# The mixing layer of a decoder block: products with tokens on partitions instead of features

## The chip, the cores and the metric

The kernel runs on one core of a Trainium2 chip. The metric is the device time of one execution in microseconds. TensorE is called PE, VectorE DVE, ScalarE ACT, GpSimdE POOL, and SyncE, which issues most transfers, SP. Each engine works through its own instructions in order.

## The reference

One decoder layer for 256 tokens of 1024 channels in float32: a feed-forward, a mixing layer, a second feed-forward, a last norm. What concerns us is the mixing layer:

```python
n = rmsnorm(h, mix_norm[l])
z = n @ w_in[l]                      # q, k, v, u, gv: 512 columns each
attn = moba_attention(q, k, v)       # one block of 256 keys: plain causal attention, 8 heads of 64
zg = gelu(z[..., 3 * A_WIDTH:])
gm = chunked_spatial_gating(u, gv, gmlp_ln_g[l], gmlp_ln_b[l], gmlp_w_s[l], gmlp_b_s[l])
                                     # u * (w_s @ layernorm(gv) + b_s) in chunks of 128 tokens, 8 groups
gates = sigmoid(n @ w_gate[l] + b_gate[l])                       # 2048 columns
merged = gates[..., :D] * (attn @ w_branch_attn[l]) + gates[..., D:] * (gm @ w_branch_gmlp[l])
h = h + merged @ w_out[l]
```

## The kernel before

Every large product is taken as three: each float32 operand is split into a rounded high part (a cast on ACT) and a remainder (a subtraction on DVE), and high x high, high x low and low x high are summed in PSUM. The weights come from DRAM in units of 1 MB, each in two halves (`raw`, seven buffers), and are split into `w` (four buffers), so a unit can be split up to three units ahead of PE. A half costs ACT one cast and DVE one subtraction of 1024 columns.

Two forms of product occur.

- Tokens stationary (`chunk`, `value`): a block of 128 features x 128 tokens is loaded, and 512 columns of weights move past it. The result has tokens on partitions. Each k-block gives three products of 512 columns for each of the two token halves. The feed-forwards, v and gv are made so.
- Weights stationary (`by_weights`, `by_passes`): a block of 128 x 128 weights is loaded and the tokens move: their high and low part together as 512 columns (`mm_high`, L165), then the high part alone, 256 columns, past the low weights (`mm_low`, L170). The result has features on partitions, in two halves of a bank; `collect` copies one on ACT and adds the other on DVE. Queries, keys, u (12 blocks of 128 features) and the gates (16 blocks) are made so, since what follows wants features on partitions.

`down_features` is the weights-stationary product that ends the first feed-forward and the mixing layer (`acc`): the last two units are taken feature block by feature block, so that DVE can add each to the residual `h`, ACT and DVE can split the next layer's input, and PE can go on with the next layer.

The factor 1/rms of each token is found late, in `token_factors`, so it is applied to the results. With features on partitions this needs a row of factors (`rows_of`, two transposes on PE) and a multiplication on DVE for each block.

PE and SP run in the order in which the program is written. ACT and DVE follow the written order inside `with in_order()` blocks (the ends of `down_features` and the start of the second feed-forward); between them a scheduler orders them. The mixing layer stands so: v, token factors, gv, queries and keys, u, scores (`sc`, L622), spatial product (`mix`, L607), 13 gate blocks, attention product (`po`), 3 gate blocks, branches (`pb`, L723 to L737), output product. The softmax's probabilities go through DRAM (`on_way`) to get keys onto partitions: `to_keys` writes them after gate block 1 and `by_keys` loads them after gate block 4.

Of the kernel before, what the change touches and what calls it, by code (L numbers as in the profile page):

```python
# [18 lines left out]
P = 128  # L19
# [26 lines left out]
def block_kernel(ctx, tc, t, out):  # L46
# [148 lines left out]
    def collect(to, ps, n=1):  # L195

        lo = tmp.tile([P, S], F32, tag="lo", name="lo")
        nc.scalar.copy(lo, ps[:, S:])
        high = ps[:, :S]
        if n > 1:  # L200
            high, lo = (x.rearrange("p (n c) -> p n c", n=n) for x in (high, lo))
        nc.vector.tensor_add(to, high, lo)

# [58 lines left out]
    def rows_of(rs, name):  # L262

        ps = bank(f"rows{name}")
        for j in range(NT):
            nc.tensor.transpose(ps[:, j * P:(j + 1) * P], rs[j].to_broadcast([P, P]), ident)
        r = small.tile([P, S], F32, tag="rows", name=f"rowsb{name}", bufs=1)
        nc.scalar.copy(r, ps[:, :S])
        return r

    def weights_of(w, nT, blk):
        c = slice(blk * P, (blk + 1) * P)
        return lambda k: ((w[:, k, 0, c], w[:, k, 1, c]), both_of(nT, k))

    def by_weights(name, i, nT, blk):

        ps, w = bank(name), unit(i, ALONE)
        by_passes([(ps, weights_of(w, nT, blk))])
        return ps

    HALVES = ((0, 512), (512, 512))

    def down_features(i0, n_units, both_of_k, scale, gain, nT, name, free, behind=()):
# [15 lines left out]
        for i in range(n_units - 2):  # L299
            unit(i0 + i, ALONE if i == n_units - 3 else PAIRED)  # L300
# [14 lines left out]
        for c in range(KB):  # L315
            blocks([c], range(K - 4, K))
# [70 lines left out]

    class Hidden:
# [22 lines left out]
        def leave(self, c):  # L411
            p, e = divmod(c, 2)
            n = 32 * self.blocks(p)
            if e == 0:
                self.way[p] = dram.tile([S, 4, n], F32, name=f"{self.name}way{p}")
            a = CH // n
            nc.sync.dma_start(self.way[p].rearrange("(j p) a n -> p j a n", p=P)[:, :, a * e:a * (e + 1), :],
                              self.turned.pop(c).rearrange("p j (a n) -> p j a n", a=a))

        def arrive(self, p):  # L420
            n = 32 * self.blocks(p)
            self.back[p] = tmp.tile([P, S // 32, n], F32, tag="back", name=f"{self.name}back{p}", bufs=1)
            way = self.way.pop(p).rearrange("(q r) a n -> r q a n", r=32)
            for a in range(4):
                nc.sync.dma_start(self.back[p][32 * a:32 * a + 32], way[:, :, a, :])

        def settle(self, p):
            n = self.blocks(p)
            to = self.aT[:, 4 * p:4 * p + n].rearrange("p k two (q c) -> p two q k c", c=32)
            split(to[:, 0], to[:, 1], self.back.pop(p).rearrange("p q (k c) -> p q k c", c=32))  # L430
# [88 lines left out]
    cols = consts.tile([P, 4 * KB], F32, name="cols")  # L519
    nc.sync.dma_start(cols, t["cols"])  # L520
    bgate, gain2, gain3 = cols[:, :2 * KB], cols[:, 2 * KB:3 * KB], cols[:, 3 * KB:]
    bs = consts.tile([P, GG // 2, P], F32, name="bs")
    for two in range(2):
        nc.sync.dma_start(bs[two * HD:(two + 1) * HD],
                            t["b_s"][two:two + 1].to_broadcast([HD, GG // 2, P]))
# [11 lines left out]
    pv, pgv = {}, {}  # L537

    def value(ps, i0, j, u):
        if u == 0:  # L540
            ps[j] = bank(f"p{units[i0][0]}{j}")
        w = unit(i0 + u)
        tk = slice(j * P, (j + 1) * P)
        for k in range(KB // 2):
            st = tuple(p[:, tk] for p in block_of(nT2, KB // 2 * u + k))
            mm3(ps[j], st, (w[:, k, 0, :], w[:, k, 1, :]), u + k == 0, u == 1 and k == KB // 2 - 1)


    with in_order():
        down_features(f1d, FB // 2, lambda k: hidden.aT[:, k], 0.5, gain2, nT2, "2", "nD", hidden.rest())  # L550
        for u in range(2):
            for j in range(NT):
                value(pv, mv, j, u)
# [3 lines left out]
        gates = mix_a[:, :2 * KB, :]  # L557
        gv = mix_a[:, 2 * KB:2 * KB + 4, :].rearrange("p (j a) t -> p j (a t)", j=NT)
        va = mix_b[:, 0:4, :].rearrange("p (j a) t -> p j (a t)", j=NT)
        uT = mix_b[:, 4:8, :]  # L560
        lng = mix_a[:, 20:22, :].rearrange("p a t -> p (a t)")
        lnb = mix_b[:, 20:22, :].rearrange("p a t -> p (a t)")
        nc.sync.dma_start(lng, t["ln_g"].to_broadcast([P, GW]))
        nc.sync.dma_start(lnb, t["ln_b"].to_broadcast([P, GW]))
        prob = [mix_b[:, 8:12, :].rearrange("p a (b n) -> p (a b) n", b=2), mix_b[:, 12:20, :]]
        for j in range(NT):
            nc.vector.tensor_scalar(va[:, j, :], pv[j], rs2[j], None, op0=ALU.mult)
    for u in range(2):
        for j in range(NT):
            value(pgv, mgv, j, u)  # L570
    rows2 = rows_of(rs2, "2")
    for j in range(NT):
        nc.scalar.activation(gv[:, j, :], pgv[j], AF.Gelu_apprx_tanh, scale=rs2[j])

    def layer_norm(j):
        st = small.tile([P, 6], F32, tag="st", name=f"st{j}")
        nc.vector.bn_stats(st, gv[:, j, :])
        mvr = small.tile([P, 2], F32, tag="mvr", name=f"mvr{j}")
        nc.vector.bn_aggr(mvr, st)
        ve = small.tile([P, 1], F32, tag="ve", name=f"ve{j}")  # L580
        nc.vector.tensor_scalar(ve, mvr[:, 1:2], EPS, None, op0=ALU.add)
        r = small.tile([P, 1], F32, tag="lnr", name=f"lnr{j}")
        nc.gpsimd.tensor_tensor(r, ve, nhalf, op=ALU.pow)
        nc.vector.tensor_scalar(gv[:, j, :], gv[:, j, :], mvr[:, 0:1], r, op0=ALU.subtract, op1=ALU.mult)
        nc.vector.tensor_mul(gv[:, j, :], gv[:, j, :], lng)
        nc.vector.tensor_add(gv[:, j, :], gv[:, j, :], lnb)

    qk = act.tile([P, 2 * (HEADS // 2), S], F32, tag="nC", name="qk")
    qT, kT = qk[:, :4], qk[:, 4:]
    for f in range(8):  # L590
        collect(qk[:, f, :], by_weights(f"pq{f}", mq + f // 2, nT2, f % 2))
        nc.vector.tensor_mul(qk[:, f, :], qk[:, f, :], rows2)
    for j in range(NT):
        layer_norm(j)

    for f in range(4):
        us = tmp.tile([P, S], F32, tag="us", name=f"uz{f}")
        collect(us, by_weights(f"pu{f}", mu + f // 2, nT2, f % 2))
        nc.vector.tensor_mul(us, us, rows2)
# [284 lines left out]
```

## Time and profile before

| | before |
|---|---|
| runs, us | 528.55, 528.67, 528.75 (median 528.67) |
| the profiled execution, us | 528.46 |
| its span in the trace, us | 526.8 |
| up to the mixing layer (0 to 186.87): PE, DVE, ACT busy, us | 185.69, 119.64, 95.55 |
| second feed-forward and end (340.68 to 526.80): PE, DVE, ACT busy, us | 179.93, 115.39, 83.20 |
| DMA in these two stages, GB/s | 258, 212 |

The span is what the trace holds from the first to the last instruction; the execution's own time lies 1.7 us above it. A row of the timeline begins with start and duration in us. A row of groups ends with count, busy us and mean ns of one, then idle time of the engine before it. A row of windows has, after the stretch and its length, the busy us of PE, weight loads, DVE, ACT and POOL, the clock granted to PE, and the DMA's share and GB/s. Rows on transfers end with their size and the us from issue to landing.

### The profile page before, as it was taken

What the parts mean: (1) busy time and instruction counts of PE and PEld (TensorE: products, weight loads), DVE (VectorE), ACT (ScalarE), POOL (GpSimd) and SP (SyncE); (2) the same over time, 40 slices, a digit from 0 to 9 for tenths busy, and PEclk for the clock granted to TensorE, in tenths of its full rate; (3) what the DMA queues carried; (4) which work ended last, traced back from release to release, by engine and by line L of the source; (5) the groups of instructions that cost most, each with busy time, mean ns of one, the idle gap of its engine ahead of it and who ended that gap; (6) DMA issues with size and microseconds to landing.
All of it is one profiled execution on the core that took longest, in us unless ns stands there. A gap on an engine that the chain in (4) does not pass through costs nothing.

```text
span 526.8 us, 7279 instructions
## 1 busy us (share of the span) xinstructions
PE 519.4 (99%) x2668; PEld 441.6 (84%) x2668; DVE 367.0 (70%) x568; ACT 273.0 (52%) x401; POOL 11.5 (2%) x20
## 2 busy tenths in 40 slices
PE   9999999999999999999999999999999999999995
PEld 6888888888888888888888998888888888888884
DVE  6886666675453689978998887799665755575424
ACT  7755354554343367547967545565444453463402
POOL 0010000000000001000000000001000000000002
PEclk9999999999999999999999999999999999999998
DMA  8999597979668229764299645259797879677302
GB/s 318 369 342 318 138 361 257 255 230 277 201 191 298 102 84 338 255 204 160 86 282 347 200 143 181 83 176 340 239 263 259 283 249 329 178 238 233 127 1 80
DMA packets 52419, 118.72 MB, mean 225 GB/s; under 512 B 6816, under 2 KB 26784, under 8 KB 52384
## 3 DMA queue, kind: packets, MB, share of 16 engines
q1 hardware_dynamic: 52096, 117.94, 68.4%
q8 instruction: 21, 0.34, 0.2%
q10 hardware_dynamic: 288, 0.33, 0.2%
q14 instruction: 14, 0.11, 0.1%
HBM read 108.81 MB, written 9.44 MB: 224 GB/s over the span
## 4 chain that ended last, share of the span: by engine, by line
PE 98%; DVE 0%; issue 0%; POOLq 0%; ACT 0%; DVEq 0%; POOL 0%; ACTq 0%
PE f L192 14%; PE f L193 14%; PE f L191 14%; PE acc L165 10%; PE pgate L165 6%; PE acc L170 5%; PE acch L193 4%; PE acch L192 4%; PE acch L191 4%; PE pgate L170 3%; PE pq L165 3%; PE pb L193 1%; PE pb L191 1%; PE pb L192 1%; PE pq L170 1%; PE pu L165 1%
## 5 line engine op out<-in xcount | busy, mean ns | idle before, releaser
L207 DVE TENSOR_TENSOR w<-raw,w 128x1024 fp32r<-128x1024 f32 x180 | 212.8, 1217 | 67.0 <-ACT w L205 66.6
L205 ACT CAST w<-raw 128x1024 fp32r<-128x1024 f32 x180 | 180.3, 1049 | 88.8 <-PE f L193 49.8
L193 PE MATMUL f<-w,n 128*128 128x512 f32 x336 | 130.7, 389 | 0.0
L192 PE MATMUL f<-w,n 128*128 128x512 f32 x336 | 130.7, 389 | 0.0
L191 PE MATMUL f<-w,n 128*128 128x512 f32 x336 | 130.7, 389 | 0.0
L191 PEld LDWEIGHTS f<-w,n 128*128 128x128 f32 x336 | 63.1, 188 | 13.2
L192 PEld LDWEIGHTS f<-w,n 128*128 128x128 f32 x336 | 63.1, 188 | 13.1
L193 PEld LDWEIGHTS f<-w,n 128*128 128x128 f32 x336 | 63.1, 188 | 13.0
L165 PE MATMUL acc<-f1h,w 128*128 128x512 f32 x176 | 43.4, 391 | 0.0
L165 PEld LDWEIGHTS acc<-f1h,w 128*128 128x128 f32 x176 | 31.9, 188 | 5.8
L191 PE MATMUL acch<-w,f2h 128*128 128x512 f32 x84 | 32.7, 389 | 0.0
L192 PE MATMUL acch<-w,f2h 128*128 128x512 f32 x84 | 32.7, 389 | 0.0
L193 PE MATMUL acch<-w,f2h 128*128 128x512 f32 x84 | 32.7, 389 | 0.0
L165 PE MATMUL pgate<-n,w 128*128 128x512 f32 x128 | 32.6, 394 | 0.0
L165 PEld LDWEIGHTS pgate<-n,w 128*128 128x128 f32 x128 | 23.0, 189 | 4.4 <-DVE mixed L629 0.2
L403 ACT ACTIVATE f2s<-f,rstd 128x256 f32<-128x256 f32 x22 | 10.3, 474 | 29.6 <-PE f L193 29.6
L405 DVE SCALAR_TENSOR_TENSOR f2a<-f,rstd,f2s 128x256 f32<-128x256 f32 x22 | 10.5, 476 | 20.9 <-ACT f2s L403 20.9
L170 PEld LDWEIGHTS acc<-f1h,w 128*128 128x128 f32 x176 | 23.5, 190 | 1.5
L170 PE MATMUL acc<-f1h,w 128*128 128x256 f32 x176 | 23.9, 282 | 0.0
L403 ACT ACTIVATE f1s<-f,rstd 128x256 f32<-128x256 f32 x22 | 10.3, 473 | 24.3 <-PE f L193 22.8
L318 DVE SCALAR_TENSOR_TENSOR h<-acc,h 128x256 f32<-128x256 f32 x32 | 13.6, 425 | 10.1 <-PE acc L165 8.1
L192 PEld LDWEIGHTS acch<-w,f2h 128*128 128x128 f32 x84 | 15.8, 188 | 3.3
(166 smaller groups left out, 634.1 us busy)
## 6 DMA issues: line engine op xcount, KB each, us to landing
raw<-in_f SPq DMA_DIRECT2D x84, 512.0 KB, 6.4
raw<-in_f1d SPq DMA_DIRECT2D x22, 512.0 KB, 6.1
raw<-in_f2d SPq DMA_DIRECT2D x22, 512.0 KB, 6.8
raw<-in_gate SPq DMA_DIRECT2D x16, 512.0 KB, 4.6
raw<-in_qk SPq DMA_DIRECT2D x8, 512.0 KB, 6.0
raw<-in_out SPq DMA_DIRECT2D x8, 512.0 KB, 4.7
f1way<-f1t SPq DMA_DIRECT2D x11, 256.0 KB, 6.7
f2way<-f2t SPq DMA_DIRECT2D x11, 256.0 KB, 6.3
```

The lines of the kernel that those rows point to most:

```text
L165: nc.tensor.matmul(ps, st, both.rearrange("p two n -> p (two n)"), start=first, stop=last)
L170: nc.tensor.matmul(ps[:, n:], st, both[:, 0, :], start=False, stop=False)
L191: nc.tensor.matmul(ps, sh, mh, start=first, stop=False)
L192: nc.tensor.matmul(ps, sh, ml, start=False, stop=False)
L193: nc.tensor.matmul(ps, sl, mh, start=False, stop=last)
L205: nc.scalar.copy(hi, src)
L207: nc.vector.tensor_sub(lo, src, hi.bitcast(F32))
L318: nc.vector.scalar_tensor_tensor(h[:, c, :], acc[c][:, q * S:(q + 1) * S], scale, h[:, c, :], op0=ALU.mult, op1=ALU.add)
L403: nc.scalar.activation(sg, ps[j][:, :CH], AF.Silu, scale=rs[j])
L405: nc.vector.scalar_tensor_tensor(a, ps[j][:, CH:], rs[j], sg, op0=ALU.mult, op1=ALU.mult)
```

## The change

All of the mixing layer's input products, and the branches, take the tokens-stationary form with 512 columns of weights moving: seven groups of 512 columns instead of 28 blocks of 128. `collect`, `rows_of`, `by_weights` and `value` go, and the token factor becomes the scale of the instruction that empties PSUM. What is needed with features on partitions is turned: DVE transposes squares of 32 x 32, the result is written to a DRAM tile, and `from_way` reads it back in four transfers, each with another order of blocks; the weights' rows and columns are permuted on the host to match. The first feed-forward's hidden values are turned in this way already (`Hidden`).

- Queries and keys: scaled on ACT, transposed, written (`qk_way`) and read back before the scores. Keys are used as they land, queries after a copy on ACT.
- Gated features: bias, multiplication with u and transpose with tokens on partitions, then `gm_way` and a split into `gmT`. The spatial product has the triangular `w_s` stationary (8 products instead of 16, each 128 columns).
- Gates: one operation on DVE (scale and bias) and a sigmoid on ACT for each 512 columns and token half.
- Merged branches: three pieces of 512, 256 and 256 columns, each multiplied with its gates, added, transposed, turned through `m_way` and split into `mT`. The first is written and read on SP, the others on ACT's queue.
- The probabilities are scaled and transposed by one instruction each for a token half instead of eight or four.
- Order: q, token factors, k, gv, u, scores, spatial, v, gate groups 0, 1, 2, attention, branch piece 0 (gated first), gate group 3, branch pieces 1 and 2, output product. The whole layer stands in `in_order()`, so ACT and DVE keep the written order too.
- `down_features` gets a count `near`: the output product takes only its last unit block by block, and the pieces' last steps run after its first and second unit. The token sums for the second feed-forward come half a chunk later.

```diff
-    mv = add_units("v", 2)
-    mgv = add_units("gv", 2)
-    mq = add_units("qk", 4)
-    mu = add_units("u", 2)
-    mg = add_units("gate", 8)
+    mq, mk, mgv, mu, mv = (add_units(name, 2) for name in ("q", "k", "gv", "u", "v"))
+    mg = add_units("gate", 6)
     mb = len(units)
-    for i in range(2):
-        units.extend([("ba", i), ("bg", i)])
+    units.extend([("bg", 0), ("ba", 0), ("gate", 6), ("gate", 7), ("ba", 1), ("bg", 1)])
...
-        for i in range(n_units - 2):
+        far = n_units - near
+        for i in range(far):
...
+    def from_way(to, way, queue=nc.sync):
+        squares32 = way.rearrange("(q r) a n -> r q a n", r=32)
+        for a in range(4):
+            queue.dma_start(to[32 * a:32 * a + 32], squares32[:, :, a, :])
...
+        def gate(g, ps):
+            c = slice(g * 512, (g + 1) * 512)
+            for j in reversed(range(NT)):
+                nc.vector.scalar_tensor_tensor(gates[:, j, c], ps[j], rs2[j], gates[:, 0, c],
+                                               op0=ALU.mult, op1=ALU.add)
+                nc.scalar.activation(gates[:, j, c], gates[:, j, c], AF.Sigmoid)
...
+        psg = chunk(mg, nT2, "g", 1, [0])
+        by_keys()
+        gm_back = tmp.tile([P, S // 32, P], F32, tag="back", name="gmback", bufs=1)
+        from_way(gm_back, gm_way)
+        chunk(mg, nT2, "g", 1, [1], psg)
+        gate(2, psg)
+        gate(1, chunk(mg, nT2, "g", 2))
...
+        settle_in(gmT, gm_back)
+        aoT, = alloc_T("ao", ("nC",))
+        for hp in range(4):
+            attend(hp)
+        for i, bT in enumerate((gmT, aoT)):
+            for j in range(NT):
+                ps = bank(f"pb{i}{j}")
+                branch(ps, ((i, ALONE), bT), j, *pieces[0])
+                m = gates[:, j, (1 - i) * D:(1 - i) * D + 512]
+                nc.vector.tensor_mul(m, ps, m)
+                if i:
+                    merged(0, j)
...
+            if p == 1:
+                settle(0)
+                leave(1)
+        from_way(m_back[1], m_way[1], nc.scalar)
+        leave(2)
+
+        def second():
+            from_way(m_back[2], m_way[2], nc.scalar)
+            settle(1)
+
+        def third():
+            settle(2)
...
-        down_features(mo, 4, lambda k: both_of(mT, k), 1.0, gain3, nT3, "3", "aT")
+        down_features(mo, 4, lambda k: both_of(mT, k), 1.0, gain3, nT3, "3", "aT", 1, [second, third])
```

ACT before, around the third gate block: a conversion of the gated features (`gm`) stands between the blocks' copies (`lo`), sigmoids (L669) and weight casts (`w`).

```order
L669 ACTIVATE mixed<-gz_2303,cols 128x256
L205 CAST gm_2300<-gm_2337 128x256
L205 CAST w_2505<-raw_0_2145 128x4x256
L198 COPY lo<-pgate_2417 128x256
L205 CAST w_2505<-raw_1_2308 128x4x256
L669 ACTIVATE mixed<-gz_2341,cols 128x256
L205 CAST gm_2300<-gm_2366 128x256
```

ACT in the changed kernel, at the end of gate group 1 (the L619 row is its two sigmoids; `gmback` is what the gated features' reads filled, `po` the attention product):

```order
L193 CAST w_2393<-raw_0_2248 128x2x512
L193 CAST w_2393<-raw_1_2283 128x2x512
L619 ACTIVATE mixed<-mixed 128x512 x2
L193 CAST gm_1771<-gmback 128x8x4x32
L193 CAST ao_2437<-po_2438 128x256
L193 CAST ao_2437<-po_2445 128x256
L193 CAST ao_2437<-po_2452 128x256
```

The four conversions of the gated features are now one, behind the sigmoids of a group that PE ends right before the attention product, whose results are converted next.

SP in the changed kernel, around the loads of the probabilities by key (`on_way`): the weight loads before them wait for buffers that DVE frees.

```order
L137 DMA raw_0_2209<-in_ba 128x1024
L587 DMA on_way_1774<-turned_2186 32x8x256 x4
L690 DMA gmway<-mixed 128x512 x2
L137 DMA raw_1_2244<-in_ba 128x1024
L137 DMA raw_0_2248<-in_gate 128x1024
L137 DMA raw_1_2283<-in_gate 128x1024
L137 DMA raw_0_2287<-in_gate 128x1024
L594 DMA mixed<-on_way_1773 128x1024
L594 DMA mixed<-on_way_1774 128x1024 x2
L362 DMA gmback<-gmway 32x8x128 x4
```

The probabilities' writes and loads keep four weight loads between them as before; the gated features' writes and reads now stand behind each.

ACT in the changed kernel, from the last branch piece into the output product (`mway` are the DRAM tiles of pieces 1 and 2, `mg` the split merged branches, the `w` casts weights of the output product):

```order
L193 CAST mg_2621<-mixed 128x8x4x32
L723 DMA mway_2431<-mt_2433 128x2x256
L362 DMA mixed<-mway_2431 32x8x64 x4
L723 DMA mway_2432<-mt_2434 128x2x256
L193 CAST w_2762<-raw_0_2511 128x1024
L193 CAST w_2762<-raw_1_2549 128x1024
L362 DMA mixed<-mway_2432 32x8x64 x4
L193 CAST mg_2622<-mixed 128x8x2x32
L193 CAST w_2809<-raw_0_2553 128x1024
L193 CAST w_2809<-raw_1_2583 128x1024
L193 CAST mg_2622<-mixed 128x8x2x32
```

Before, ACT issued no transfer here; now ten of them stand in its queue among the casts.

More of the change, by code (lines that the diff above doesn't have):

```diff
@@ L260, in token_factors, with down_features @@
         return [r[:, j:j + 1] for j in range(NT)]
[L262 to L279, printed above, removed]
     HALVES = ((0, 512), (512, 512))
-    def down_features(i0, n_units, both_of_k, scale, gain, nT, name, free, behind=()):
+    def down_features(i0, n_units, both_of_k, scale, gain, nT, name, free, near, behind):
         acc = [bank(f"acc{name}{c}") for c in range(KB)]
@@ L315, in down_features @@
         for c in range(KB):
-            blocks([c], range(K - 4, K))
+            blocks([c], range(2 * far, K))
             for q in range(2):
@@ L535, in block_kernel @@
     nT2 = alloc_T("n2", ("nA", "nB"))
[L537 to L546, printed above, removed]
     with in_order():
[L550 to L553, printed above, removed]
+        down_features(f1d, FB // 2, lambda k: hidden.aT[:, k], 0.5, gain2, nT2, "2", "nD", 2, hidden.rest())
+        psq = chunk(mq, nT2, "q", 0)
         rs2 = token_factors("2")
@@ L556, in block_kernel, with tokens @@
         mix_a, mix_b = mixed[:, :FB], mixed[:, FB:]
[L557 to L562, printed above, removed]
+        def tokens(blocks):
+            return blocks.rearrange("p (j a) t -> p j (a t)", j=NT)
@@ new lines, in block_kernel @@
+        gates = tokens(mix_a[:, :2 * KB])
+        gv, va, ut = tokens(mix_a[:, 16:20]), tokens(mix_b[:, 0:4]), tokens(mix_b[:, 4:8])
+        lng, lnb = (mix[:, 20:22].rearrange("p a t -> p (a t)") for mix in (mix_a, mix_b))
+        prob = [mix_b[:, 8:12, :].rearrange("p a (b n) -> p (a b) n", b=2), mix_b[:, 12:20, :]]
+        gmT, = alloc_T("gm", ("nD",))
+        gm_way, gm_turned = dram.tile([S, 4, P], F32, name="gmway"), (lng, lnb)
+        on_way = [dram.tile([(j + 1) * P, 4, S], F32, name=f"on_way{j}") for j in range(NT)]
@@ L569, in block_kernel @@
+        psu = chunk(mu, nT2, "u", 0, [0])
         for j in range(NT):
[L570 to L599, printed above, removed]
-        nc.scalar.activation(uT[:, f, :], us, AF.Gelu_apprx_tanh)
@@ new lines, in block_kernel @@
+        scores(0)
+        scores(1)
+        spatial()
+        psv = chunk(mv, nT2, "v", 0, [0])
+        nc.sync.dma_start(gates[:, 0, :], t["b_gate"].to_broadcast([P, 2 * D]))
+        sums = [exponents(j) for j in range(NT)]
+        for j in range(NT):
+            gated(j, 0)
+        probabilities(0, sums[0])
+        chunk(mv, nT2, "v", 0, [1], psv)
+        to_keys(0)
+        probabilities(1, sums[1])
+        for j in range(NT):
+            gated(j, 1)
+            nc.vector.tensor_scalar(va[:, j, :], psv[j], rs2[j], None, op0=ALU.mult)
@@ new lines, in block_kernel @@
+        chunk(mb + 2, nT2, "g", 0, [1], psg)
+        from_way(m_back[0], m_way[0])
+        gate(3, psg)
+        mT = alloc_T("mg", ("nA", "nB"))
+        for p in (1, 2):
+            c0, n = pieces[p]
+            for j in range(NT):
+                ps = bank(f"pb{c0}{j}")
+                for q, bT in enumerate((aoT, gmT)):
+                    branch(ps[:, q * n:(q + 1) * n], ((4 + q, PAIRED), bT), j, c0, n)
+                m = gates[:, j].rearrange("p (q c) -> p q c", q=2)[:, :, c0:c0 + n]
+                nc.vector.tensor_mul(m, ps.rearrange("p (q c) -> p q c", q=2), m)
+                merged(p, j)
+            if p == 1:
+                settle(0)
+                leave(1)
```

309 lines of the change are left out of this document (161 added, 148 removed).

## The prediction

> **What bounds the kernel now.** I read the page's busy times first, then the chain that ended last, then the stage that the change rewrites.
>
> ```profile
> span 526.8 us, 7279 instructions
> PE 519.4 (99%) x2668; PEld 441.6 (84%) x2668; DVE 367.0 (70%) x568; ACT 273.0 (52%) x401; POOL 11.5 (2%) x20
> PE 98%; DVE 0%; issue 0%; POOLq 0%; ACT 0%; DVEq 0%; POOL 0%; ACTq 0%
> 186.87:340.68 153.81, 153.81 (x965) 136.32 (x964) 131.95 (x246) 94.21 (x172) 2.90 (x3) 1.00 0.60 202
> ```
>
> PE works 519.4 of 526.8 us and is 98% of the chain. The last row is the mixing layer, from its first product (v) to the first product of the second feed-forward: 153.81 us, PE busy in all of it, DVE in 131.95, ACT in 94.21, the DMA at 0.60 of its share. Nothing is hidden behind PE that could be shortened with profit. The time can fall only by PE instructions that go, or go faster, and rises with each PE wait that the new order brings. So I count PE by its rows and then look for waits.
>
> **PE, part by part.** In the chain in order of time each piece begins where the one before has issued; differences of starts are what PE pays.
>
> ```profile
> 186.87 0.23 PE pv L191
> 197.78 0.23 PE sums L247
> 198.02 0.23 PE pgv L191
> ...
> 209.11 1.60 PE pq L165 x7
> ...
> 242.62 2.82 PE sc L622 x32
> 245.44 1.90 PE mix L607 x32
> 247.34 1.83 PE pgate L165 x7
> ...
> 283.88 0.59 PE po L692 x4
> ...
> 286.68 1.81 PE pgate L165 x7
> 295.04 0.23 PE pgate L165
> ...
> 318.31 2.75 PE acc L165 x12
> 340.68 0.23 PE f L191
> ...
> 351.59 0.23 PE sums L247
> ```
>
> Queries, keys and u (209.11 to 242.62) take 33.51 us, the gates 36.54 and, from 286.68 to the first branch product at 295.27 (295.04 + 0.23), 8.59: 78.64 us for 28 blocks of 128 features, each eight 512-column and eight 256-column products. With tokens stationary the same work is 7 groups of 48 products of 512 columns. The row of that form is v, 10.91 from 186.87 to 197.78, or the first chunk of the second feed-forward, 340.68 to 351.59, 10.91 too. 7 x 10.9 = 76.3: **-2.3 us**. The gain is per instruction: a 512-column product costs 10.9/48 = 0.227 us, eight of 256 columns 0.96, so 0.12 each, and two of those are 0.24.
>
> The transposes of the token factors (the stretch from the end of gv, 198.02 + 10.9 = 208.9, to 209.11) go: **-0.2**.
>
> The branches go from 23.04 (295.27 to 318.31, 192 products of 256 columns, 0.120 each) to 48 of 512 columns and 96 of 256: 10.9 + 11.5 = 22.4, **-0.6**.
>
> The spatial product goes from 32 passes to 16 of the same 128 columns, but its stationary tile grows from 64 to 128 columns.
>
> ```profile
> L607 PEld LDWEIGHTS mix<-wsT,mixed 128*64 128x64 f32 x32 | 1.7, 137 | 0.3 <-DVE w L207 0.3
> L193 PEld LDWEIGHTS pb<-gm,w 128*128 128x128 f32 x32 | 6.0, 189 | 0.0
> ```
>
> At the old pace (1.90/32 = 0.059) 16 passes are 0.95 us; at the pace of the branch's 128-column loads (0.120) they are 1.9. Sixty-four more columns lengthen a load by 189 - 137 = 52 ns, so about 104 ns for 128; I take 16 x 0.104 = 1.6, **-0.3**, and keep 0 and -0.95 as ends. Scores (2.82), attention (2.80), the token sums and the output product (22.37) keep their instructions; only the order of the last changes. Sum: **-3.4**, ends -3.1 and -4.1.
>
> **Where PE may now wait.** Carried forward from 186.87 with these numbers, the groups begin: k 198.0, gv 208.9, u 219.8, scores 230.7, spatial 233.5, v 235.1, gate group 0 246.0, group 1 256.9, group 2 267.8, attention 278.7, its end 281.5, the first branch piece till 292.4, gate group 3 till 303.3, the other pieces till 314.9, output product till 337.2.
>
> *Gated features.* Before, ACT converted them between gate blocks, far ahead of the branches. Now ACT's order puts their conversion behind the two sigmoids of gate group 1, and those end on the group whose last product ends at 278.7. Their rows:
>
> ```profile
> 186.91 0.88 DVE L318 SCALAR_TENSOR_TENSOR h<-acc,h 128x256 f32<-128x256 f32 x2
> 205.61 1.41 DVE L567 TENSOR_SCALAR mixed<-pv,rstd 128x512 f32<-128x512 f32 x2 [0.60 <-POOL rstd L259]
> 207.62 0.69 ACT L573 ACTIVATE mixed<-pgv,rstd 128x512 f32<-128x512 f32 x1
> 66.71 1.05 ACT L205 CAST f1h<-f1back 128x1024 fp32r<-128x1024 f32 x1
> 67.99 1.22 DVE L207 TENSOR_TENSOR f1h<-f1back,f1h 128x1024 fp32r<-128x1024 f32 x1
> ```
>
> DVE starts 0.04 after a group's end (186.91 against 186.87). Bias additions of 512 columns: 0.7 each. First sigmoid from 0.8 to 1.5, second till 2.15, conversion 1.05, high half at 3.2; DVE's remainder 1.2, low half at 4.4, which PE sees at 4.45. PE has the attention products (2.8) and two products of the high half (0.45) to do meanwhile: it waits 4.45 - 3.25 = **+1.2 us**. If each of the five steps ends 0.15 sooner, as back-to-back rows do (1.41 for two of 0.7 and over), it is 0.5; if each adds as much, 2.0. Queued behind on ACT are the four conversions of the attention output (0.4 each), needed 5.4 us later than the gated ones, and weight splits needed at 298: they cost nothing.
>
> *VectorE between scores and gate group 1.* From the first scores (232) its queue holds, by the old rows:
>
> ```profile
> 245.21 1.94 DVE L629 TENSOR_TENSOR mixed<-sc,mask 128x512 f32<-128x512 f32 x4
> 250.06 2.27 DVE L644 TENSOR_REDUCE mx<-mixed 128x8 f32<-128x2048 f32 x1
> 259.41 2.71 DVE L660 STREAM_TRANSPOSE turned<-mixed 128x256 f32<-128x256 f32 x8
> 262.36 0.41 DVE L700 TENSOR_TENSOR mixb<-mix,bs 128x256 f32<-128x256 f32 x1
> ```
>
> Masks 2.7 (six additions at that row's rate), maxima 3.8 (2.27 for 2048 columns, half for 1024, two short ones), scaling and turning of the probabilities 2.6 and 4.8 (one instruction of 2048 columns like the reduction's), twelve operations of 0.41 for the gated features, 5.0, v 1.4, weights 2.3 + 2.3 and half a unit 1.2: 26.1 us, and about 1.5 of waiting for ACT's exponentials: 259.6. The second half of gate group 1 needs that half unit at 262.4, so 2.8 us are spare: nothing.
>
> *Probabilities.* The three loads by key stand on SP behind a weight load that waits for the last split before them, about 268.4.
>
> ```profile
> 271.08 1.40 SPq L684 DMA_DIRECT2D mixed<-on_way  x3
> mixed<-on_way SPq DMA_DIRECT2D x3, 512.0 KB, 7.5
> f1back<-f1way SPq DMA_DIRECT2D x4, 64.0 KB, 6.4
> f2back<-f2way SPq DMA_DIRECT2D x4, 64.0 KB, 2.0
> f2way<-f2t SPq DMA_DIRECT2D x11, 256.0 KB, 6.3
> ```
>
> Issued by 269.9 and landing 7.5 later: 277.4, needed 278.7. Nothing; another 1.2 would hide in the wait for the gated features. Behind them on SP are the gated features' reads, needed by ACT only at 280.9, and weights for 298. Queries and keys have more: the keys' group ends at 208.9, is scaled and turned by about 212 (2 x 0.7 on ACT, as much on DVE, a weight split between), written from 214, landed 6.3 later (f2way), read back behind two weight loads by 227, needed 230.7.
>
> *Merged branches.* Piece 0 leaves on SP after 292.4 and is needed at 314.9: two transfers of 6 to 7 us, the splits of 2 and the weight loads between them fit. Pieces 1 and 2 leave and return on ACT's queue, whose instructions wait there for the landing of the write before and so hold the weight splits behind them. Write of piece 1 at 2.7 before the output product starts (314.9), four reads of 0.45 after its landing, write of piece 2, its landing, four reads, then the conversion of piece 1 (1.3 with DVE): with a landing of L it is ready at 2.2 + 2L after the start, and needed at two units, 11.2. It costs nothing up to L = 4.5. By my working SP issues hardly a weight load from 309 to 321, so the nearest row is the quiet one, 2.0 for the kernel's last reads: nothing.
>
> *Output product's end.* Only its last unit is now taken block by block: PE ends a block each 22.37/32 = 0.70 us where DVE needs about 1.3 (0.88 for two additions, half that for the remainder). DVE falls some 5 us behind, but the chunk that follows takes a block each 10.9/8 = 1.36 us and finds each ready; the token sums, which would be late, are moved half a chunk on. Nothing.
>
> **Sum.** -3.4 + 1.2 = -2.2. From the profiled execution, 528.46, that is 526.3; from the median of the runs, 528.67, which is 0.2 higher, 526.5. I say **526.4**.
>
> **Rivals.**
> 1. *No wait for the gated features, and loads that keep the old pace* (the quicker end of each bound): -4.1 + 0.5: 525.0, or 524.5 with no wait. For it: the scores' 128-column loads already run at 2.82/32 = 0.088 a pass. Against: ACT's five steps depend on each other. Chance 0.2.
> 2. *VectorE or the probabilities late.* The weights of gate group 1, or the keys, 1 to 2 us beyond their spare time: -2.2 + 1.5 = about 528, no change to speak of. For it: DVE was busy 131.95 of 153.81 and now runs in a fixed order. Against: both terms have spare time by the rows, and longer instructions replace many short ones. Chance 0.18.
> 3. *The merged pieces' way through DRAM becomes the bound: slower.* At the landing of a busy queue, L = 6.3, piece 1 is 2 x (6.3 - 4.5) = 3.6 us late and piece 2, ready at 2.2 + 3L, another 0.7: -2.2 + 4.3, 530.7. It decides from L = 5.6 (no net gain), and the kernel is slower by more than 0.2% from about 6.1. For it: 64 KB reads took 6.4 us under load. Against: the queue is nearly empty there. The Trainium skill, "DMA: Bandwidth & Descriptors", Specifications, names 512 B as the least transfer for full rate; pieces 1 and 2 are read in runs of 256 B. The f2back row, of such runs, landed in 2.0 us, so here the rule costs nothing by itself. Chance 0.1.
> 4. *The wider products gain next to nothing.* Their gain rests on the part of a product's time that doesn't grow with its columns: 0.227 against 0.24 for two halves, some 10 ns. The rows have it in both forms, 0.351 us before and 0.341 after for 768 columns. Were it 2 ns, the -2.3 would shrink to -0.3 and the sum to -0.2: 528.4, the same. The rows speak against it. Chance 0.03. The Trainium skill, "TensorE: Matmul & The Clock Gate", Back-to-back issue gap, gives N / 2.4 + 2.5 ns for an isolated product, which is this case; the trace's 227 and 120 ns don't agree with its 216 and 109, and the measurement decides.
>
> **How the numbers follow.** My forecast, between 525.2 and 527.6, has 0.49. Rival 1 lies below, 2 and 4 around 528, 3 above. The range leaves out rival 3 and little else: 524.3 to 528.9. About 0.2% (1.06 us) is what a measurement can tell from no change. Faster by that, below 527.6: forecast 0.46, rival 1 0.2, a little of rival 2 (0.04): 0.70. Within: 0.18. Slower: 0.12, rival 3 and the far end of rival 2.
>
> **What would show it.** Groups of q, k, u and gates at 10.9 us each; the spatial product near 1.6; a PE gap of about 1.2 before the first branch product, ended by the gated features' low half, and no other over 0.3 from 186.9 on; f starting near 338.4 rather than 340.7. PE gaps before the keys' attention, before gate group 1's second half, or within the output product would make it wrong, in that order of likelihood; so would groups slower than 10.9.

## The result, and the profile after

The changed kernel takes 533.76 us (median of 5 runs, 532.71 to 535.24), the one before 528.55 beside it (5 runs, 528.48 to 528.75). The ratio is 1.010, with an interval from 1.0079 to 1.012: **slower by 5.2 us**, where the prediction had 2.3 us faster and a range that ended at 528.9. The profiled execution took 533.1.

The page, after: span, busy times, the granted clock in 40 slices, and the shares of the chain that ended last.

```profile
span 531.4 us, 6830 instructions
PE 520.0 (98%) x2490; PEld 435.1 (82%) x2490; DVE 357.9 (67%) x490; ACT 263.4 (50%) x359; POOL 12.2 (2%) x20
PEclk9999999999999999999997999999999999999998
PE 87%; DVE 4%; DMA 4%; ACT 2%; issue 1%; POOLq 0%; DVEq 0%; SPq 0%; POOL 0%; ACTq 0%
```

PE was 98% of the chain before; now DMA, DVE and ACT stand in it, and one slice ahead of the last (about 279 to 292 us) has a lower clock. PE's waits in the mixing layer, after (us in total, times, longest):

```profile
PE po L627 <- DMA mixed<-on_way: 2.8, 1, 2.8
PE po L629 <- DMA mixed<-on_way: 1.0, 1, 1.0
PE pb L190 <- DVE gm L195: 0.4, 1, 0.4
```

The last is the predicted wait for the gated features; the other two, for the probabilities loaded by key, were predicted not to be there. The chain in order of time shows what lies under them, after (start, us, what):

```profile
257.78 4.62 DVE w L195 x4
...
267.85 0.26 SPq L137
268.20 8.43 DMA raw<-in_gate
276.65 10.88 DMA gmback<-gmway
287.69 1.05 ACT gm L193
288.76 1.24 DVE gm L195
290.05 0.50 PE pb L190
```

Read from below: the third branch product (the first on the low half) starts at 290.05, because the gated features landed at 287.6; their last read was issued only at 276.65, when a weight load had landed. ACT stood idle meanwhile (after; in brackets the idle time before a row and what ended it):

```profile
280.75 0.63 ACT L619 ACTIVATE mixed<-mixed 128x512 f32<-128x512 f32 x1 [0.16 <-DVE mixed L617]
287.69 1.04 ACT L193 CAST gm<-gmback 128x1024 fp32r<-128x1024 f32 x1 [6.31 <-DMA gmback<-gmway]
```

Gate group 1 had ended at 279.0, so without a wait that product would start at 282.3, after 2.83 us of attention and two products. **PE loses 7.8 us here**, where 1.2 were predicted. Of these, 4.2 are the three waits above. Most of the rest is attention itself, which ran from 281.98 to 288.88, a wait of 1.0 included, instead of 2.83 us, at half the clock (windows, after; last three columns: granted clock, DMA share, GB/s):

```profile
283.00:285.00 2.00, 1.05 (x8) 0.79 (x9) 0.00 (x0) 0.00 (x0) 0.00 (x0) 0.50 1.08 235
285.00:287.00 2.00, 2.00 (x16) 1.81 (x14) 0.00 (x0) 0.00 (x0) 0.00 (x0) 0.50 1.05 239
```

SP's queue, after, shows how the reads came to be so late:

```profile
259.02 0.35 SPq L137 DMA_DIRECT2D raw<-in_bg  x1
260.15 0.35 SPq L137 DMA_DIRECT2D raw<-in_ba  x1
260.56 3.98 SPq L587 DMA_DIRECT2D on_way<-turned  x4
264.58 2.27 SPq L690 DMA_DIRECT2D gmway<-mixed  x2
266.95 0.66 SPq L137 DMA_DIRECT2D raw<-in_ba  x1
267.70 1.39 SPq L137 DMA_DIRECT2D raw<-in_gate  x3
269.14 2.64 SPq L594 DMA_DIRECT2D mixed<-on_way  x3
271.82 5.13 SPq L362 DMA_DIRECT2D gmback<-gmway  x4
```

The turned probabilities were ready at 254.1 (L582 ends there), but two weight loads stand ahead of their write, and those wait for buffers that VectorE, at the softmax and the gating, has not split yet: the view of SP's waits has

```profile
SPq L137 <- DVE w L195: 18.0, 5, 9.8
```

Once VectorE splits again (257.78), everything is issued close together, from 259 to 277, and the transfers land late (size, us to landing, after):

```profile
mixed<-on_way SPq DMA_DIRECT2D x3, 512.0 KB, 11.6
gmback<-gmway SPq DMA_DIRECT2D x4, 128.0 KB, 11.7
```

The same loads by key took 7.5 us before. The windows, after, show the idle time and the burst behind it:

```profile
256.00:260.00 4.00, 4.00 (x20) 3.30 (x19) 3.93 (x6) 0.00 (x0) 0.00 (x0) 1.00 0.03 11
260.00:264.00 4.00, 4.00 (x19) 3.32 (x18) 3.81 (x5) 0.75 (x2) 0.00 (x0) 1.00 0.84 229
264.00:278.00 14.00, 14.00 (x63) 11.60 (x62) 9.94 (x10) 9.65 (x11) 0.00 (x0) 1.00 0.99 336
278.00:288.00 10.00, 6.20 (x34) 4.29 (x34) 2.47 (x3) 1.57 (x3) 0.00 (x0) 0.68 1.08 254
```

The DMA engines move next to nothing from 256 to 260, while the data to be moved lie there, and are full for the 24 us from 264 to 288. Full engines alone don't make a late landing: before, in the same two stretches, they were nearly as full, and no transfer held PE.

```profile
264.00:278.00 14.00, 14.00 (x82) 12.33 (x82) 14.00 (x31) 9.20 (x20) 0.00 (x0) 1.00 0.95 298
278.00:288.00 10.00, 10.00 (x72) 8.43 (x71) 9.13 (x16) 7.97 (x16) 0.00 (x0) 1.00 0.94 347
```

### The profile page after: what moved, and what is told of

It is laid out like the page before. It is cut to its first block, busy times and chain, and to the rows that moved or that the text cites. A ratio compares the mean times of both kernels' runs of the same rounds, so it can differ in the third digit from the quotient of the medians.

```text
span 531.4 us, 6830 instructions
## 1 busy us (share of the span) xinstructions
PE 520.0 (98%) x2490; PEld 435.1 (82%) x2490; DVE 357.9 (67%) x490; ACT 263.4 (50%) x359; POOL 12.2 (2%) x20
## 4 chain that ended last, share of the span: by engine, by line
PE 87%; DVE 4%; DMA 4%; ACT 2%; issue 1%; POOLq 0%; DVEq 0%; SPq 0%; POOL 0%; ACTq 0%
PE f L190 14%; PE f L188 14%; PE f L189 14%; PE acc L162 10%; PE acc L167 5%; PE acch L190 4%; PE acch L188 4%; PE acch L189 4%; DMA gmback<-gmway 2%; DMA raw<-in_gate 2%; DVE w L195 2%; PE pb L190 1%; PE pb L189 1%; PE pb L188 1%; ACT mixed L569 1%
## 5 line engine op out<-in xcount | busy, mean ns | idle before, releaser
L188 PE MATMUL g<-w,n 128*128 128x512 f32 x64 | 24.9, 389 | 0.0
L189 PE MATMUL g<-w,n 128*128 128x512 f32 x64 | 24.9, 389 | 0.0
L190 PE MATMUL g<-w,n 128*128 128x512 f32 x64 | 24.9, 389 | 0.0
```

What stands on the lines that cost most here:

```text
L188: nc.tensor.matmul(ps, sh, mh, start=first, stop=False)
L189: nc.tensor.matmul(ps, sh, ml, start=False, stop=False)
L190: nc.tensor.matmul(ps, sl, mh, start=False, stop=last)
```

## Experiments

Theories at the start. A: the turned tiles' place in SP's queue makes them late. B: the gated features alone do. C: the DMA engines are at their limit, so that whatever is issued last is late. Each row: median (lowest to highest) and ratio to the kernel before with its interval, then, of the profiled execution, when attention and the third branch product start.

| run | us | ratio | attention | third product |
|---|---|---|---|---|
| after | 533.8 (532.7–535.2) | 1.0100 (1.0079–1.0120) | 282.0 | 290.1 |
| e1_keys_pool | 528.0 (527.1–531.1) | 0.9993 (0.9978–1.0008) | 278.9 | 283.5 |
| e2_gated_pool | 527.9 (527.0–532.9) | 0.9998 (0.9977–1.0019) | 279.6 | 284.2 |
| e3_both_pool | 533.4 (533.0–533.8) | 1.0087 (1.0072–1.0102) | 279.1 | 287.9 |
| e4_sp_order | 531.0 (528.2–534.2) | 1.0039 (1.0018–1.0060) | 279.0 | 285.1 |
| e5_fill | 531.2 (530.9–531.7) | 1.0049 (1.0036–1.0062) | 279.0 | 287.1 |
| e6_gated_first | 533.2 (531.3–534.5) | 1.0089 (1.0071–1.0107) | 280.9 | 288.3 |
| e7_convert_early | 531.2 (530.9–533.1) | 1.0056 (1.0044–1.0068) | 281.3 | 289.6 |
| e8_sp_reads_first | 534.3 (533.1–536.3) | 1.0108 (1.0093–1.0124) | 279.4 | 289.6 |
| e9_long_runs | 534.1 (532.7–535.3) | 1.0103 (1.0087–1.0119) | 281.5 | 289.5 |
| e10_nine_buffers | 533.7 (533.1–534.7) | 1.0097 (1.0084–1.0110) | 283.2 | 290.9 |
| e11_half_group | 529.7 (528.9–531.7) | 1.0027 (1.0018–1.0037) | 284.9 | 290.6 |
| e12_gated_early | 534.1 (533.2–534.4) | 1.0101 (1.0088–1.0114) | 279.3 | 288.6 |
| e13_and_converted | 530.5 (527.7–531.9) | 1.0025 (1.0011–1.0039) | 279.6 | 285.3 |
| e14_two_less_ahead | 534.9 (532.8–535.2) | 1.0103 (1.0087–1.0120) | 279.5 | 289.9 |
| e15_two_queues | 527.4 (526.8–529.3) | 0.9982 (0.9972–0.9991) | 279.0 | 283.5 |
| e16_two_queues_conv | 527.1 (525.5–529.5) | 0.9973 (0.9959–0.9986) | 280.7 | 284.1 |
| e17_split_one_ahead | 529.7 (528.2–533.5) | 1.0027 (1.0009–1.0046) | 279.1 | 283.6 |

**Another queue for one of the two ways (e1, e2), or both (e3, e6, e7).** POOL's queue is all but empty in this stage.

```diff
+        to_keys(1, nc.gpsimd)          # e1; e3 too
+        by_keys(nc.gpsimd)
+        for j in range(NT):            # e2; e3 too
+            nc.gpsimd.dma_start(by_token(gm_way)[:, j], gm_turned[j])
+        from_way(gm_back, gm_way, nc.gpsimd)
         psg = chunk(mg, nT2, "g", 0, [0])
```

> Only the second block's turned probabilities and the three loads by key go to POOL's queue, where nothing stands ahead of them; the gated features stay on SP. Theory A (place in SP's queue): the writes go from 254.1, the loads by key land by about 270, attention starts at 279.0 with its group's end instead of 282.0, and it keeps its full clock (2.8 us instead of 6.9). SP, relieved of seven issues, sends the gated features' reads about 4 us sooner, so they land by 283 instead of 287.6 and the first branch product waits about 1 to 3 us: 527 to 529 us. Theory B (the gated features alone are what ends last, and SP's relief does nothing for them): the low half still comes at 290.0, about 533. Theory C (the DMA engines are at their limit, wherever a transfer is issued): landings stay at 11 us and more, the keys come in time all the same, the gated features as in B: 533.

> Only the gated features' write and reads go to POOL's queue, from 257.3; the keys' loads stay on SP behind the weights. Theory A: the gated features are there by 275, but the keys still land at 281 to 284 and attention runs at a lowered clock till about 288.5: only the 0.7 us before the first branch's third product go, 532.5 to 533. Theory B (the gated features alone matter): 526.5. Theory C: about 533.

> Both ways through DRAM go to POOL's queue, in the order in which their tiles are ready. Theory A: no wait but the 1.2 us of the predicted conversion behind the sigmoids: 526 to 527. Theory B: the same 526.5. Theory C (engines at their limit): the transfers take 11 us and more, but from 261 on they still land before 279, unless the weights beside them come late: 526 to 531 with waits at weight splits in gate groups 1 and 2.

Each alone takes away the loss against the kernel before: 528.0 and 527.9. For e1 A had it right, and B and C fall. For e2 A was wrong by 5 us, and B was nearer: the keys landed at 280.8 (attention starts at 279.6 and waits 0.5 us), not at 284. SP issued the loads by key no sooner than in the changed kernel (268.9 against 269.1); with the gated features' way out of the burst, they landed in 8.7 us instead of 11.6. Both together are as slow as the change: POOL's queue is in order too, the second half of the gated features' write stood behind loads by key that waited for a landing, their reads went at 275.1, and they landed at 285.4. With the gated features ahead instead (e6), the loads by key were issued at 267.7 and were late; e7, with the conversion ahead of the sigmoids, waited for the same keys, so its difference to e6 says nothing on the conversion.

> Both ways on POOL's queue, the gated features' write and reads now ahead of the three loads by key. If the place in a queue decides: gated features landed by about 272, keys by 277, no PE wait but the predicted one for the conversion behind the sigmoids (1.2 us): third branch product at 283.3 to 283.5, 526.8 (the profiled execution of before, 528.5, less the 2.9 us that PE saves by the first runs' traces, plus 1.2). If the engines' load decides, the keys take the place of what is late: attention waits 1 to 3 us, 528 to 531.

> As the run before, and the gated features' conversion stands ahead of the two last sigmoids of gate group 1 on ACT and of their two additions on DVE. If the predicted wait of 1.2 us is as the prediction has it: it goes, 525.6. If the wait comes from the landing: no change against the run before, or worse, since now the sigmoids wait too.

**The slow stretch behind a wait (e5).** In e3 the first branch products took 0.43 us instead of 0.227. e5 is e3 with filler:

```diff
+        fill = bank("fill")
+        for i in range(40):
+            nc.tensor.matmul(fill[:, :S], zeros[:, :P], zeros, start=True, stop=True)
         for i, bT in enumerate((gmT, aoT)):
```

> As the run with both ways on POOL's queue (533.4), where PE stood idle for 4.7 us between attention and the first branch and then took 0.43 us instead of 0.227 for each product till 291; here 40 small products on zeros (added work, some 0.11 us each, whose result nobody reads) fill that gap. If the slow stretch comes from PE's idleness: products at 0.227 from the first one on, about 2.3 us less, 531.0. If it comes from something else (the burst of DMA traffic beside it): 533.4 as before. If the fill only delays: 534.

Windows of e3, then of e5: PE's gap, and the stretch behind it.

```profile
281.90:286.50 4.60, 0.04 (x1) 0.00 (x0) 0.00 (x0) 1.00 (x2) 0.00 (x0) 0.75 0.98 273
286.60:291.00 4.40, 4.36 (x9) 2.98 (x10) 4.40 (x7) 2.92 (x6) 0.00 (x0) 0.50 0.05 18
```

```profile
281.90:286.50 4.60, 4.60 (x42) 4.03 (x41) 0.66 (x1) 1.74 (x4) 0.00 (x0) 1.00 0.95 283
286.60:291.00 4.40, 4.08 (x18) 3.21 (x18) 4.40 (x8) 2.20 (x4) 0.00 (x0) 1.00 0.12 42
```

PE idle for 4.7 us gets a clock of 0.50 for the next 4.4 us and does 9 products there; kept busy with useless products it keeps 1.00 and does 18, and **the kernel with more work is 2.1 us faster** (531.2 against 533.4). The DMA burst is the same in both gaps (share 0.98 and 0.95), so it is not the cause. The Trainium skill, "TensorE: Matmul & The Clock Gate", Part 1, has the clock halved after an idle window of about 3.4 us and again full after as long a busy one; the wait of 4.7 us agrees, while the slow stretch of 4.4 us is longer. Shorter waits brought it too: the changed kernel's 2.85 us ahead of attention (a clock of 0.50 from 282.0 on), and in e4 waits of 1.9 and 0.5 us with two products between; in e13 waits of 1.4 and 0.7 did not. There the measurement decides.

**All on SP, in another order (e4, e8, e14).** The writes stand ahead of the weight loads in all three; e8 also has both kinds of reads ahead of the next weights, e14 fetches two half units less ahead.

```diff
+        to_keys(1)                                   # e4, e8
+        for j in range(NT):
+            nc.sync.dma_start(by_token(gm_way)[:, j], gm_turned[j])
         psg = chunk(mg, nT2, "g", 0, [0])
+        by_keys()                                    # e4, e8
+        from_way(gm_back, gm_way)                    # e8
```

> All transfers stay on SP; the second block's turned probabilities and the gated features are written ahead of the weight loads that stood before them, and the loads by key stand before the last weights' loads of gate group 0 rather than behind them. Theory A: writes at 254 to 260 instead of 260.6 to 266.9, keys landed by about 275 to 277, gated features by 280: 526.5 to 528, with the predicted 1.2 us of waiting. Theory C: landings stretch to 12 us and the weight loads that now stand behind come late: PE waits at gate group 1 or 2, and 529 to 533.

> All on SP: writes ahead of the weight loads, then the loads by key and the gated features' reads together, and only then the next weights' loads. If the order of transfers decides: reads issued by 267, landed by 278 even at 11 us, 526.8 with the conversion's 1.2 us. If the weights that now stand behind are needed: a PE wait in gate group 2 or at the first branch, ended by a weight's split, 529 and more.

> The changed kernel, all on SP, where the weights are fetched five half units ahead instead of seven from the first gate group to the gated features' reads: the writes then stand ahead of the weight loads, no weight load waits for a buffer there, and 1 MB less of weights stands ahead of the loads by key. If the backlog ahead of the turned tiles is the cause: loads by key issued by 265 and landed by 275, gated features landed by 279, weights in time, 527 to 528. If the engines' load in all is: the weights that come later are late in turn (PE waits at the first branch, ended by a weight's split), 530 to 534.

Attention is on time in all of them, and still they take 531.0, 534.3 and 534.9. In e4 it is again a landing: the gated features' reads went from 268.6 on and took 11.0 us, and ACT waited 0.9 us for them; behind PE's waits of 1.9 and 0.5 us the clock was 0.50. In e8 the first guess, that the DMA engines have too much to do (C), is not what ACT's timeline shows:

```profile
280.39 1.05 ACT L193 CAST w<-raw 128x1024 fp32r<-128x1024 f32 x1 [6.78 <-DMA raw<-in_ba]
281.74 1.04 ACT L193 CAST w<-raw 128x1024 fp32r<-128x1024 f32 x1 [0.30 <-DMA raw<-in_gate]
282.95 1.04 ACT L193 CAST w<-raw 128x1024 fp32r<-128x1024 f32 x1 [0.17 <-DMA raw<-in_gate]
285.94 0.63 ACT L619 ACTIVATE mixed<-mixed 128x512 f32<-128x512 f32 x1 [1.95 <-DVE mixed L617]
286.73 0.63 ACT L619 ACTIVATE mixed<-mixed 128x512 f32<-128x512 f32 x1 [0.16 <-DVE mixed L617]
287.27 1.03 ACT L193 CAST gm<-gmback 128x1024 fp32r<-128x1024 f32 x1
```

The conversion of the gated features waits for nothing of its own. It stands behind the sigmoids, these behind additions on DVE, and these behind splits of weights up to three units ahead, which now land late and which PE needs only behind the first branch product (in e15, where nothing is late, at about 290 and from 294 on). e14 shows the same: ACT waits 7.75 us for a weight load, and the conversion begins at 287.55. e17 is e8 with one edit:

```diff
-        gate(1, chunk(mg, nT2, "g", 2))
+        gate(1, chunk(mg, nT2, "g", 2, ahead=ALONE - 2))
```

> As the run in which SP alone issues the loads by key and the gated features' reads ahead of the next weights (534.3; PE waited 6.1 us for a conversion that ACT began at 287.3), with one edit: gate group 2's chunk splits weights one unit ahead instead of three. If ACT's and VectorE's fixed order held the conversion behind splits whose weights came late: the conversion starts with the features' landing or behind the sigmoids at about 281, 527 to 528. If the features themselves landed that late: 534 as before. If the weights of the second branch are then late: a PE wait of 1 to 3 us at it, 529 to 531.

ACT's timeline of e17:

```profile
279.95 0.63 ACT L619 ACTIVATE mixed<-mixed 128x512 f32<-128x512 f32 x1 [7.56 <-DVE mixed L617]
280.73 0.63 ACT L619 ACTIVATE mixed<-mixed 128x512 f32<-128x512 f32 x1 [0.15 <-DVE mixed L617]
281.27 1.03 ACT L193 CAST gm<-gmback 128x1024 fp32r<-128x1024 f32 x1
283.26 7.72 ACT L193 CAST w<-raw 128x1024 fp32r<-128x1024 f32 x8
```

The conversion begins at 281.27 instead of 287.27 and the third product at 283.6 instead of 289.6. The time falls by 4.6 us, not by the 6 to 7 expected: in the profiled execution (528.4) the output product waits 1.4 us for piece 0 of the merged branches. What made other runs of e17 longer, up to 533.5, no trace shows.

**Weights, runs and cover (e9, e10, e11, e12, e13).** e9 is e3 with the gated features read in runs of 2 KB and left in another order than the products need; e10 has `RAW = 9`; e11 is e1 with the first half of gate group 3 ahead of attention; e12 is e1 with the gated features written on SP ahead of two weight loads and read ahead of two more, e13 is e12 with their conversion ahead of the last sigmoids.

> As the run with both ways on POOL's queue (533.4, gated features landed at 285.4 and alone what ends last), but the four reads of the gated features bring the same bytes in runs of 2 KB instead of 512 B; they then lie in another order than the products need, so the gated branch's values are wrong. In the windows in which those reads run the engines are full but move 170 to 240 GB/s instead of 410. If the short runs are what takes the engines' time: the reads land about 3 us sooner, PE waits some 1.7 us instead of 4.7, 529.5 to 531. If the low rate comes from two queues that share the engines: 533.4 as before.

> The changed kernel with nine buffers for fetched half units of weights instead of seven, in the whole kernel. In the changed kernel the engines move nothing from 246 to 249 and from 256 to 260, because all seven buffers hold weights that VectorE, at the softmax, has not split, and are full from 264 to 292. If this burst is the cause: two half units (1 MB, 2.5 us at 410 GB/s) are fetched before it, the gated features land about 2.5 us sooner, 531.3. If the transfers' place in SP's queue alone decides: no change, 533.8; with more weights ahead of them in the queue, 534 to 535.

> As the run with the keys on POOL's queue (528.0), and the first half of gate group 3 (24 products, 5.45 us) stands ahead of attention instead of behind the first branch piece, with its weights fetched ahead of the branches'; the four attention products lie in two PSUM banks instead of four. The work is the same. If the waits are for landings that come at a time of their own: attention starts at 284.4, the gated features are there at 283, no PE wait is left, f starts at 337.7 to 338.0 and the time is 525.5 to 526. If the engines' backlog simply moves (weights of the half group needed sooner, the gated features behind them): a PE wait at the half group or at the first branch again, 527 to 529.

> As the run with the keys on POOL's queue (528.0; PE still waited 1.2 us for the gated features, whose write stood on SP behind two weight loads and landed at 270.8), with the gated features written ahead of those loads and read ahead of two more. If the engines serve all of the 7.6 MB by 281 wherever they stand, and only the order of what is last differs: gated features landed by 277, and the conversion behind the sigmoids is what is left, the predicted 1.2 us: third branch product at 283.3 to 283.5, no gain, 527.5 to 528.3. If weights take the last place: a wait of 2 us and more with a slow stretch behind it, 530 to 533.

> As the run before, with the gated features' conversion ahead of the last two sigmoids of gate group 1. If the predicted wait is right as a mechanism: with the features landed by 277 it goes, third branch product at 282.3, 526.5 (f at 337.8). If the landing is what decides: the sigmoids wait behind it, as long as before or longer, 528 to 530.

In e9 and e10 the hoped-for gain didn't come. Longer runs brought the landing from 7.6 to 6.8 us; PE waited 3.8 us instead of 4.7, in a run whose scores had waited too. Two more buffers are filled ahead of the burst, but the fetches then run two halves further ahead within it, and nothing is gained. In e11 no landing holds PE at the branch any more; what it gains goes to two new waits, 1.9 us for a shared bank between attention products and 0.8 for piece 0 of the merged branches. e12 holds keys and gated features in time and is as slow as the change, by the order on ACT that e8 shows; e13, where the conversion no longer stands behind the sigmoids, is 3.6 us faster with the same transfers; it still stands behind the cast of a weight that landed at 281.8.

**Both links mended (e15, e16).** Writes of the probabilities and all of the gated features' way on POOL, loads by key on SP behind two weight loads, and splits two units ahead at gate group 2:

```diff
+            to_keys(1, nc.gpsimd)
...
+            from_way(gm_back, gm_way, nc.gpsimd)
         psg = chunk(mg, nT2, "g", 0, [0])
+        by_keys()
...
-        gate(1, chunk(mg, nT2, "g", 2))
+        psg = chunk(mg, nT2, "g", 2, ahead=ALONE - 1)
+        settle_in(gmT, gm_back)                      # here in e16 alone
+        gate(1, psg)
```

> The second block's turned probabilities are written, and the gated features written and read, on POOL's queue; the loads by key stand on SP behind two weight loads; and gate group 2's chunk splits weights two units ahead instead of three, so that no split of a unit needed later (gate group 3's) stands ahead of gate group 1's additions and sigmoids on VectorE and ACT. If in the runs with early reads (534.3, 534.1, 534.9) those splits, waiting for their late weights, held the conversion of features that had landed: features landed by 273, keys by 274, nothing held; only the predicted 1.2 us for the conversion behind the sigmoids: third branch product at 283.3 to 283.6, 526.8. If the landings themselves are late: a wait of 2 us and more, 529 to 534.

> As the run before, with the gated features' conversion ahead of the last two sigmoids of gate group 1 and their additions. If the predicted wait for the conversion is right: it goes, third branch product at 282.3, f at 337.8, 525.6 (1.2 us less than the run before). If the conversion was not what PE waited for: no difference to the run before.

The chain of e15 in order of time, at the first branch:

```profile
279.87 0.76 DVE mixed L617
280.86 0.34 issue
281.19 1.04 ACT gm L193
282.25 1.24 DVE gm L195
283.53 0.50 PE pb L190
```

No transfer is left in it. The third product starts at 283.53, as expected, and the profiled execution takes 526.83 (expected 526.8). e15 is faster than the kernel before by 0.18% (0.09 to 0.28) and e16 by 0.27% (0.14 to 0.41). In e16's profiled execution the wait for the conversion is gone (the third product follows attention at once), but the scores wait 0.9 us for the keys and the output product 1.2 for piece 0; its lowest run, 525.54, is the time expected. So the 1.2 us seem to be there to be had, and in the profiled execution they are lost to the next landings; no trace of the lowest run was kept. e15's windows beside those of after: the idle stretch is used, and the burst is over sooner.

```profile
256.00:260.00 4.00, 4.00 (x19) 3.34 (x18) 3.93 (x7) 0.00 (x0) 2.15 (x4) 1.00 0.94 225
278.00:288.00 10.00, 9.05 (x59) 6.91 (x58) 7.86 (x11) 7.08 (x11) 0.00 (x0) 1.00 0.70 273
```

## Why the prediction was wrong

**The step that failed** is *Probabilities*: "Issued by 269.9 and landing 7.5 later: 277.4, needed 278.7. Nothing", with the sentence behind it on the gated features' reads, "needed by ACT only at 280.9". The issue was nearly right (269.1 to 271.8). The landing was not: 7.5 us was taken from the old schedule, and here it was 11.6, so that attention waited 2.8 and 1.0 us, the first of the signs that the prediction names for being wrong. The gated features' reads were given no landing at all: issued from 271.8 to 276.7 and landing 11.7 later, they came at 287.6, when ACT had stood idle for 6.3 us. They ended last, and with them the loss at the branch is 7.8, 6.6 above the predicted 1.2. The two can't be added up: the late keys, with the lower clock behind them, held PE till 289.6 (290.05 less the last wait of 0.43) by themselves. The sum had no term for the clock at all. e1, e2 and e15 show it from the other side: with the landings in time, or nearly so, the loss goes.

Why the landing grew from 7.5 to 11.6 is shown only in part. From 262 to 290 about as much was moved as before (8.48 MB against 8.40). But from the probabilities' write up to their loads by key SP issued 3.5 MB in 8.6 us, against 3.0 in 8.9 before, and the gated features' reads came right behind. In e2, with 3.0 MB ahead again and these reads gone from the queue, the landing was 8.7. How much each of the two adds, no run separates.

**What the runs showed in its place** is a chain of queues in order. VectorE's softmax holds the weights' buffers; weight loads that wait for them hold SP, and with it tiles ready since 254; then all is issued at once. Where the turned tiles were put first on SP, the weights came late and held VectorE and ACT, which split them long before PE needs them, and with them the sigmoids and the conversion (e8 and e17). The DMA engines' load in all is no bound: e15 moves the same bytes without a wait for a landing at the branch.

**Rival 2**, VectorE or the probabilities late, named the right kind of wait and gave it 1 to 2 us. Its price left out that the gated features stand behind the probabilities in the same queue.

**PE's sum** of -3.4 was nearly right. f starts at 338.97 in e15 against 340.68 before; with the 1.27 us of its wait (283.53 against 282.26) that is -3.0. Each group takes 10.9 us as predicted (q from 186.83 to 197.74). The missing 0.4 us: the scores take 2.98 instead of 2.82 (230.55 to 233.53), the spatial product 1.81 instead of 1.6 (233.53 to 235.34), and the branches some 0.2 more than 22.4. (By the prediction's own rows 16 x 0.104 is 1.66, and six masks on VectorE are 2.9 instead of 2.7; neither decides anything.)

**The wait for the gated features**, +1.2, is right: e15 has 1.27, by the steps the prediction lists. **VectorE between scores and gate group 1**: no PE wait there, as predicted. **Queries and keys**: the prediction had them back by 227; in the profile after, the keys' reads are issued at 221.6 to 223.0 and land 7.4 later, just at the scores' start of 230.55, and in the profiled executions of e9, e10 and e16 the scores wait 0.9 to 1.5 us. This, too, is a landing taken too short. **Merged branches**: no cost in the changed kernel, and its ACT queue was as quiet as predicted (2.4 to 2.6 us), so rival 3 did not come; but piece 0, on SP, has no room to spare: once PE comes earlier it waits 0.8 to 1.4 us (e11, e16, e17).

Add up: 526.3 from the profiled execution, plus 6.6 for the late landings and the lower clock that came with them, plus 0.4 for PE's sum, gives 533.3; it took 533.1.

## What to carry to other kernels

A transfer's time to landing belongs to the schedule in which it was measured: when a change adds transfers or lets an engine hold back the loads ahead of them, add up what stands ahead of it in its queue at the new place and allow for more than the old time, or issue the transfer from a queue of its own as soon as its data are ready. Follow a late landing through every engine that works in order: work for later units that stands ahead of work for the next one turns a harmless delay into a PE wait. A sequence in which PE was 98% of the chain has no spare time by itself; each tile that newly goes through DRAM needs its cover counted from the write to the landing of the last read.

## What was not expected of the hardware

- After waits of 2.4 us (e4, in two parts) to 6.3 us (e14) PE ran at a clock of 0.50 for some 4 to 7 us, so a wait of 4.7 us cost 2.1 us more; 40 useless products took this away (e5).
- At a DMA share of 1.08, 254 GB/s were moved from 278 to 288 in the profile after; before, at a share of 0.94, it was 347. In the slow time the gated features' four reads into 32 partitions each were in flight. Runs of 2 KB instead of 512 B (e9) shortened their landing by only 0.8 us; what limits them stays open.
- The time varies more from run to run than before: 532.7 to 535.2 for the changed kernel and 527.0 to 532.9 for e2, where the kernel before spans 528.4 to 529.5 in all its runs. That varying landing times are the reason is likely, but each kernel has one trace, so it is not shown.
